# A row-mean kernel read in tiles: 126 rows a partition in place of 127, and a second block of 128 rows behind the second tile

## The chip, the cores and the metric

The kernel runs on one core of one Trainium2 chip. The metric is device time in microseconds of the whole program; a profile's span is about 1.3 us shorter (159.8 us for a run of 161.13 us in the kernel before). The engines in the profile are DVE (VectorE), ACT (ScalarE), POOL (GpSimd) and SP (SyncE, which issues the DMA transfers); TensorE does nothing here.

## The reference

```python
batch, seq, dim = 32, 512, 1024           # x: 16384 rows of 1024 float32, 64 MiB
def reference(x):
    return np.mean(np.maximum(x, 0), axis=-1).astype(np.float32)
```

Each row of 4 KB becomes one number. There is one pass over 64 MiB and next to no output (64 KB).

## The kernel before

The first 128 rows are a block by themselves, one row a partition. The other 16256 are dealt out 127 to a partition, so that a partition's rows are contiguous in HBM. They come in seven tiles of 16 rows a partition, then in ever smaller pieces (7, 4, 2, 1 rows, and the last row in three pieces of columns), so that little work is left behind the last byte. Three buffers take the tiles in turn.

```python
xfirst, xmain = xf[:P, :], xf[P:, :]
J = J - 1                                            # 127
xr = xmain.rearrange("(p j) d -> p j d", p=P, j=J)
NB, BUFS = 16, 3
row_pieces, col_pieces = [7, 4, 2, 1], [512, 256, 256]
# ... cut ...
for t in range(full):                                # full = 7, on SP
    buf_free(t)            # from t = 3 on: ACT and DVE are through with tile t - 3
    if t == 0:
        load(-1, row0[:, :], xfirst)
    load(t, bufs[t % BUFS][:, :, :], xr[:, t * NB:(t + 1) * NB, :])
    if t == BUFS:
        nc.sync.wait_ge(first, 2)
        nc.sync.dma_start(
            out=outfirst.rearrange("(q i) -> q i", i=32), in_=turned0[0:P:32, :],
        ).then_inc(stored, 16)
# ... cut: loads of the row and column pieces ...
def rows(i, xt, lo, n, j0):
    nc.scalar.wait_ge(loaded[i], 16)
    nc.vector.wait_ge(loaded[i], 16)
    for k in range(lo, lo + n):
        j = j0 + k
        done = (dve_row if j % 2 else act_row)(nc, xt[:, k, :], sums[:, j:j + 1])
        # ... cut: the last two rows of a tile count up dve and act ...
# ... cut ...
nc.scalar.wait_ge(loaded[-1], 16)
nc.scalar.activation(
    out=row0[:, :], in_=row0[:, :], func=ACT.Relu, scale=inv, accum_out=mean0[:, 0:1],
).then_inc(first, 1)
nc.vector.wait_ge(first, 1)
nc.vector.transpose(turned0[:, :], mean0[:, :]).then_inc(first, 1)
for t in range(full):
    rows(t, bufs[t % BUFS], 0, NB, t * NB)
```

Odd rows go to DVE and even rows to ACT, each with one instruction that takes the maximum with 0 and sums up (for a row, 1.22 us on DVE and 1.04 us on ACT in the profile before). The means of the block lie one in each partition; a transpose of 32 x 32 blocks (0.21 us on DVE) turns them into four rows of 32 numbers, which a small store of 4 x 128 B writes out (four packets of 128 B in the trace).

## Time and profile before

| what | before |
|---|---|
| time, median of the first 3 runs (lowest to highest) | 161.34 us (161.02 to 161.39) |
| span of the profiled run | 159.8 us |
| busy: DVE, ACT | 46%, 44% |
| HBM read | 67.11 MB, 420 GB/s over the span |
| from tile to tile (8.39 MB) | 19.34 to 19.36 us, 433 GB/s |
| last DVE operation starts | 157.84 us |

The prediction shows the lines that carry this. In the DMA row each digit is a fortieth of the span in tenths busy; in a group's line, the figures behind the second bar are the engine's idle time ahead of that group and what ended it. In a line of the timeline, square brackets hold the engine's wait just before the instruction and what ended it. One more view belongs in front: what SP issued, in order. Columns are start, length, engine and line, operation, what is written from what, and how many were merged. The first three lines show the block, then tiles 0 to 3, then the small store behind tile 3 (tiles count from 0); the last shows the final store.

```profile
0.00 0.39 SPq L109 DMA_DIRECT2D row<-in_x_dram  x1
0.45 32.18 SPq L109 DMA_DIRECT2D rows<-in_x_dram  x4
32.68 0.64 SPq L125 DMA_DIRECT2D out_dram<-turned  x1
...
158.30 0.34 SPq L208 DMA_DIRECT2D out_dram<-res  x1
```

### The profile page before, as it was taken

What the parts mean: (1) busy time and instruction counts of PE and PEld (TensorE: products, weight loads), DVE (VectorE), ACT (ScalarE), POOL (GpSimd) and SP (SyncE); (2) the same over time, 40 slices, a digit from 0 to 9 for tenths busy, and PEclk for the clock granted to TensorE, in tenths of its full rate; (3) what the DMA queues carried; (4) which work ended last, traced back from release to release, by engine and by line L of the source; (5) the groups of instructions that cost most, each with busy time, mean ns of one, the idle gap of its engine ahead of it and who ended that gap; (6) DMA issues with size and microseconds to landing.
All of it is one profiled execution on the core that took longest, in us unless ns stands there. A gap on an engine that the chain in (4) does not pass through costs nothing. (4 is left out here: it accounts for less than half of the span.)

```text
span 159.8 us, 348 instructions
## 1 busy us (share of the span) xinstructions
DVE 73.3 (46%) x131; ACT 70.4 (44%) x133; POOL 1.3 (1%) x9
## 2 busy tenths in 40 slices
DVE  0000029900399005970079500894009920199975
ACT  1400029800397005950079300892009900199974
POOL 1000000000000000000000000000000000000001
DMA  9979989999799699699699699799899997998993
GB/s 394 459 328 525 410 377 525 394 394 525 345 443 525 263 525 525 263 525 525 263 525 509 279 525 476 312 525 427 361 525 394 394 525 328 427 438 382 414 411 110
DMA packets 2456, 67.18 MB, mean 420 GB/s; under 512 B 536, under 2 KB 792, under 8 KB 1176
## 3 DMA queue, kind: packets, MB, share of 16 engines
q1 hardware_dynamic: 2456, 67.18, 97.9%
HBM read 67.11 MB, written 0.07 MB: 420 GB/s over the span
## 5 line engine op out<-in xcount | busy, mean ns | idle before, releaser
L20 DVE TENSOR_SCALAR_CACHE_REDUCE rows<-rows 128x1024 f32<-128x1024 f32 (+1 forms) x63 | 72.1, 1209 | 78.8 <-DMA rows<-in_x_dram 78.6
L15 ACT ACTIVATE rows<-rows 128x1024 f32<-128x1024 f32 x64 | 66.2, 1035 | 84.0 <-DMA rows<-in_x_dram 83.8
L15 ACT ACTIVATION_READ_ACCUMULATOR rows<-rows 128x1 f32 x64 | 11.9, 186 | 0.0
L20 DVE DVE_READ_ACCUMULATOR rows<-rows 128x1 f32 x63 | 5.2, 83 | 0.0
L168 DVE STREAM_TRANSPOSE turned<-mean 128x32 f32<-128x32 f32 x1 | 0.2, 211 | 5.9 <-ACT row L164 5.9
L164 ACT ACT_TABLE_LOAD x1 | 1.3, 1283 | 3.3 <-DMA row<-in_x_dram 3.3
L157 POOL TENSOR_SCALAR res<-sums 128x112 f32<-128x112 f32 (+1 forms) x2 | 0.5, 249 | 153.8 <-DVE rows L20 153.8
L164 ACT ACTIVATE row<-row 128x1024 f32<-128x1024 f32 x1 | 1.1, 1056 | 0.0
L15 ACT ACTIVATE last<-last 128x512 f32<-128x512 f32 x1 | 0.6, 629 | 0.0
L20 DVE TENSOR_SCALAR_CACHE_REDUCE last<-last 128x256 f32<-128x256 f32 x1 | 0.4, 420 | 0.3 <-DMA last<-in_x_dram 0.3
L197 DVE SCALAR_TENSOR_TENSOR last<-last,scale 128x258 f32<-128x258 f32 x1 | 0.4, 428 | 0.1
L142 POOL MEMSET scale<- 128x258 f32 x1 | 0.3, 313 | 0.0
L187 POOL TENSOR_SCALAR res<-part 128x1 f32<-128x1 f32 x1 | 0.3, 266 | 0.6 <-DVE rows L20 0.6
L164 ACT ACTIVATION_READ_ACCUMULATOR row<-row 128x1 f32 x1 | 0.2, 187 | 0.0
L15 ACT ACTIVATION_READ_ACCUMULATOR last<-last 128x1 f32 x1 | 0.2, 186 | 0.0
L141 POOL MEMSET mean<- 128x32 f32 x1 | 0.1, 125 | 1.5 <-POOLq L55 1.5
L235 POOL MEMSET const-bfloat16-1.0<- 128x1 bf16 x1 | 0.1, 103 | 0.0
L235 POOL MEMSET const-uint8-127<- 128x1 uint8 x1 | 0.1, 103 | 0.0
L235 POOL MEMSET const-float32-0.0<- 128x1 f32 x1 | 0.1, 99 | 0.2 <-issue 0.2
L235 POOL MEMSET const-float32-1.0<- 128x1 f32 x1 | 0.1, 99 | 0.0
L20 DVE DVE_READ_ACCUMULATOR last<-last 128x1 f32 x1 | 0.1, 83 | 0.0
L197 DVE DVE_READ_ACCUMULATOR last<-last,scale 128x1 f32 x1 | 0.1, 82 | 0.0
## 6 DMA issues: line engine op xcount, KB each, us to landing
rows<-in_x_dram SPq DMA_DIRECT2D x1, 3584.0 KB, 37.9
rows<-in_x_dram SPq DMA_DIRECT2D x1, 2048.0 KB, 42.4
rows<-in_x_dram SPq DMA_DIRECT2D x1, 1024.0 KB, 44.5
row<-in_x_dram SPq DMA_DIRECT2D x1, 512.0 KB, 3.2
rows<-in_x_dram SPq DMA_DIRECT2D x1, 512.0 KB, 45.3
last<-in_x_dram SPq DMA_DIRECT2D x1, 256.0 KB, 45.5
last<-in_x_dram SPq DMA_DIRECT2D x2, 128.0 KB, 45.2
rows<-in_x_dram SPq DMA_DIRECT2D x7, 48.7
```

The costliest lines, as they stand in the source:

```text
L15: return nc.scalar.activation(out=src, in_=src, func=ACT.Relu, accum_out=acc)
L20: return nc.vector.tensor_scalar(out=src, in0=src, scalar1=0.0, scalar2=init, op0=ALU.max, op1=ALU.add, accum_out=acc,)
L141: nc.gpsimd.memset(mean0[:, :], 0.0)
L142: nc.gpsimd.memset(scale[:, :], inv).then_inc(pool, 1)
L157: nc.gpsimd.tensor_scalar(out=res[:, lo:hi], in0=sums[:, lo:hi], scalar1=inv, scalar2=0.0, op0=ALU.mult, op1=ALU.add,).then_inc(pool, 1)
L164: nc.scalar.activation(out=row0[:, :], in_=row0[:, :], func=ACT.Relu, scale=inv, accum_out=mean0[:, 0:1],).then_inc(first, 1)
L168: nc.vector.transpose(turned0[:, :], mean0[:, :]).then_inc(first, 1)
L187: nc.gpsimd.tensor_scalar(out=res[:, J - 2:J - 1], in0=part[:, 0:1], scalar1=part[:, 1:2], scalar2=inv, op0=ALU.add, op1=ALU.mult,).then_i ...
L197: nc.vector.scalar_tensor_tensor(out=last[:, 768:], in0=last[:, 768:], scalar=0.0, in1=scale[:, :], op0=ALU.max, op1=ALU.mult, accum_out=r ...
L235: nc = _bacc.Bacc("TRN2", target_bir_lowering=False, num_devices=1)
```

## The change

A second block of 128 rows is taken out of the front, so 126 rows a partition remain (504 KiB from one partition's rows to the next in HBM, before 508 KiB). The second block is loaded behind tile 1 and worked on by ACT between tiles 1 and 2. The first tail piece has 6 rows in place of 7, the last store 14 columns in place of 15, and there are two small stores, behind tile 5.

```diff
-    xfirst, xmain = xf[:P, :], xf[P:, :]
-    J = J - 1
+    xfirst, xmain = xf[:2 * P, :].rearrange("(c p) d -> p c d", c=2), xf[2 * P:, :]
+    J = J - 2
-    row_pieces = [7, 4, 2, 1]
+    row_pieces = [6, 4, 2, 1]
     for t in range(full):
         buf_free(t)
-        if t == 0:
-            load(-1, row0[:, :], xfirst)
+        if t in (0, 2):
+            c = t // 2
+            load(c - 2, row0[:, c, :], xfirst[:, c, :])
         load(t, bufs[t % BUFS][:, :, :], xr[:, t * NB:(t + 1) * NB, :])
-        if t == BUFS:
+        if t == BUFS + 2:
             nc.sync.wait_ge(first, 2)
-            nc.sync.dma_start(... one store of 4 x 32 ...).then_inc(stored, 16)
+            for c in range(2):
+                nc.sync.dma_start(... one store of 4 x 32 ...).then_inc(stored, 16)
     for t in range(full):
+        if t in (0, 2):
+            c = t // 2
+            nc.scalar.wait_ge(loaded[c - 2], 16)
+            done = nc.scalar.activation(
+                out=row0[:, c, :], in_=row0[:, c, :], func=ACT.Relu, scale=inv, accum_out=mean0[:, c:c + 1],
+            )
+            if c == 1:
+                done.then_inc(first, 1)
+                nc.vector.wait_ge(first, 1)
+                nc.vector.transpose(turned0[:, :], mean0[:, :]).then_inc(first, 1)
         rows(t, bufs[t % BUFS], 0, NB, t * NB)
# ... cut: the same activation and transpose removed from ahead of the loop;
#     one semaphore more; the wait for all stores is 64 in place of 48 ...
```

More of the change, by code (lines that the diff above doesn't have):

```diff
@@ L63 @@
     inv = 1.0 / D
-    xfirst, xmain = xf[:P, :], xf[P:, :]
-    outfirst, outmain = out.flatten()[:P], out.flatten()[P:]
-    J = J - 1
+    xfirst, xmain = xf[:2 * P, :].rearrange("(c p) d -> p c d", c=2), xf[2 * P:, :]
+    outfirst, outmain = out.flatten()[:2 * P], out.flatten()[2 * P:]
+    J = J - 2
     xr = xmain.rearrange("(p j) d -> p j d", p=P, j=J)
@@ L88 @@
     scale = sbuf("scale", P, D // 4 + 2)
-    row0, mean0, turned0 = sbuf("row0", P, D), sbuf("mean0", P, 32), sbuf("turned0", P, 32)
-    loaded = [nc.alloc_semaphore(f"loaded{i}") for i in range(full + len(row_pieces) + len(col_pieces) + 1)]
+    row0, mean0, turned0 = sbuf("row0", P, 2, D), sbuf("mean0", P, 32), sbuf("turned0", P, 32)
+    loaded = [nc.alloc_semaphore(f"loaded{i}") for i in range(full + len(row_pieces) + len(col_pieces) + 2)]
     act, dve, pool = (nc.alloc_semaphore(n) for n in ("act", "dve", "pool"))
@@ L118 @@
         buf_free(t)
-        if t == 0:
-            load(-1, row0[:, :], xfirst)
+        if t in (0, 2):
+            c = t // 2
+            load(c - 2, row0[:, c, :], xfirst[:, c, :])
         load(t, bufs[t % BUFS][:, :, :], xr[:, t * NB:(t + 1) * NB, :])
-        if t == BUFS:
+        if t == BUFS + 2:
             nc.sync.wait_ge(first, 2)
-            nc.sync.dma_start(
-                out=outfirst.rearrange("(q i) -> q i", i=32), in_=turned0[0:P:32, :],
-            ).then_inc(stored, 16)
+            for c in range(2):
+                nc.sync.dma_start(
+                    out=outfirst[c * P:(c + 1) * P].rearrange("(q i) -> q i", i=32), in_=turned0[c:P:32, :],
+                ).then_inc(stored, 16)
     j0 = full * NB
@@ L162 @@
     nc.vector.wait_ge(pool, 1)
-    nc.scalar.wait_ge(loaded[-1], 16)
-    nc.scalar.activation(
-        out=row0[:, :], in_=row0[:, :], func=ACT.Relu, scale=inv, accum_out=mean0[:, 0:1],
-    ).then_inc(first, 1)
-    nc.vector.wait_ge(first, 1)
-    nc.vector.transpose(turned0[:, :], mean0[:, :]).then_inc(first, 1)
-    for t in range(full):
+    for t in range(full):
+        if t in (0, 2):
[8 more added lines that the diff above has]
+                nc.vector.transpose(turned0[:, :], mean0[:, :]).then_inc(first, 1)
         rows(t, bufs[t % BUFS], 0, NB, t * NB)
@@ L212 @@
     nc.sync.sem_clear(range(used[0], used[-1] + 1))
-    nc.sync.wait_ge(stored, 48).then_inc(stored, -48)
+    nc.sync.wait_ge(stored, 64).then_inc(stored, -64)
     for e, hint in zip(hinted, hints):
```

## The prediction

The sum came to +0.10 us (161.34 + 0.10, stated as 161.45). One of the two grounds for its 0.08 us is the one-row piece of the tail, 1.28 us behind the piece before it where its bytes take 1.21, so read the 0.08 as the author's estimate from this 0.07. The "6.5 us around it" are 161.34 less the 154.8 us of the input. The 16 and the 8 in the packet count are worked out from the trace before: it has 276 packets of 4 B, which comes to 16 for each of the 15 loads and the two stores of 128 packets, and 4 for the small store, beside that store's 4 of 128 B.

> **What bounds the kernel now.** I read the page from the top, then the waits, then the busy time between tile arrivals, then the last four microseconds of the timeline. The page first: neither compute engine is half used, the DMA row is full from the first slice to the last but one, and both compute groups spend more time waiting for rows than working on them.
>
> ```profile
> span 159.8 us, 348 instructions
> DVE 73.3 (46%) x131; ACT 70.4 (44%) x133; POOL 1.3 (1%) x9
> DMA  9979989999799699699699699799899997998993
> ...
> DMA packets 2456, 67.18 MB, mean 420 GB/s; under 512 B 536, under 2 KB 792, under 8 KB 1176
> ...
> L20 DVE TENSOR_SCALAR_CACHE_REDUCE rows<-rows 128x1024 f32<-128x1024 f32 (+1 forms) x63 | 72.1, 1209 | 78.8 <-DMA rows<-in_x_dram 78.6
> L15 ACT ACTIVATE rows<-rows 128x1024 f32<-128x1024 f32 x64 | 66.2, 1035 | 84.0 <-DMA rows<-in_x_dram 83.8
> ```
>
> The reader is to see 78.6 us of idle DVE and 83.8 us of idle ACT, all ended by the arrival of x. The kernel is a stream of 64 MiB, and the engines keep up. The chain of waits (the page's part 4) names only the last DVE instruction, because a landing is not an instruction, so it doesn't help here.
>
> Next, busy time by stage, with the cuts put where each tile of 16 rows a partition is first touched, that is, where it landed:
>
> ```profile
> 22.99:42.35 19.36, 9.21 (x16) 8.42 (x16) 0.00 (x0) 1.00 1.00 433
> 42.35:61.71 19.36, 9.21 (x17) 8.43 (x17) 0.00 (x0) 1.00 1.00 433
> 61.71:81.05 19.34, 9.21 (x16) 8.42 (x16) 0.00 (x0) 1.00 1.00 434
> 81.05:100.40 19.35, 9.21 (x16) 8.42 (x16) 0.00 (x0) 1.00 1.00 434
> ```
>
> The columns are the stretch, its length, busy time of DVE, ACT and POOL with counts, the granted clock, the DMA share and GB/s. Each tile is 128 x 16 x 4096 B = 8.39 MB, and 8.39 MB / 19.355 us = 433.4 GB/s with a DMA share of 1.00: not one gap between tiles. One row a partition (512 KiB) therefore costs 19.355 / 16 = 1.210 us of stream, and the whole input 128 x 1.210 = 154.8 us out of a time of 161.34. What is left is the start (first bytes), the work behind the last bytes, the last store, and some 1.3 us outside the span (the profiled run had a span of 159.8 and a time of 161.13).
>
> Last, the end of the timeline (start, length, engine, operation):
>
> ```profile
> 152.51 1.22 DVE L20 TENSOR_SCALAR_CACHE_REDUCE rows<-rows 128x1024 f32<-128x1024 f32 x1 [0.77 <-DMA rows<-in_x_dram]
> ...
> 156.29 0.75 DVE L20 TENSOR_SCALAR_CACHE_REDUCE rows<-rows 128x576 f32<-128x576 f32 x1
> ...
> 157.32 0.42 DVE L20 TENSOR_SCALAR_CACHE_REDUCE last<-last 128x256 f32<-128x256 f32 x1 [0.27 <-DMA last<-in_x_dram]
> ...
> 157.84 0.43 DVE L197 SCALAR_TENSOR_TENSOR last<-last,scale 128x258 f32<-128x258 f32 x1
> 158.19 0.08 DVE L197 DVE_READ_ACCUMULATOR last<-last,scale 128x1 f32 x1
> 158.30 0.34 SPq L208 DMA_DIRECT2D out_dram<-res  x1
> ```
>
> Right up to the last column pieces DVE waits for data (0.77 us before the piece of four rows, 0.27 us before the columns 512 to 767). Behind the last bytes come one short DVE operation, the issue of the store (0.34 us) and 1.0 us until it has landed.
>
> [...] tiles become usable in the order of issue, 19.34 to 19.36 us apart.
>
> **The change part by part.** (1) Bytes of x: unchanged. Before: 1 block row + 7 x 16 + 7 + 4 + 2 + 1 + 1 = 128 rows a partition. After: 1 + 32, 1, 5 x 16, then 6 + 4 + 2 + 1 + 1 = 128. So 0 us of stream added or removed.
>
> (2) Order: block two sits in the queue behind tile 1 and ahead of tile 2. Tiles 2 to 6 land 1.21 us later each (61.71 becomes about 62.9, 139.12 about 140.3), and the shortened piece (6 rows in place of 7) gives it all back: its last byte is number 120 of 128 in both kernels, so everything from 147.6 us on lands when it did. 0 us.
>
> (3) One more load in the stream, 128 packets of 4 KB[...]. What a separate DMA costs beyond its bytes I take from two places: [...] the one-row piece of the tail, which starts 156.29 - 155.01 = 1.28 us behind the piece before it in place of 1.21, 0.07 more. I add 0.08 us on the path.
>
> (4) Compute: ACT still does 64 block or whole rows (62 even rows and 2 blocks, before 63 and 1), DVE still 62, and one transpose of 0.21 us each. Block two costs ACT 1.06 us, between tile 1 and tile 2, where it idles 10.93 us. DVE waits for it and for the transpose there, and idles 10.15 us. Nothing on the path. Releases of buffers do not move, as tile 1's rows come first.
>
> (5) The tail on DVE. Tile 6 now lands at about 140.4. Eight rows at 1.14 us start to start (139.12, 140.26, ...) end at 149.5; three rows of the piece of six end at 152.9, against a landing of the next piece at 152.5 to 152.6, so the wait of 0.77 us vanishes. Two rows end at 155.2 (landed at 155.1), one at 156.4 (the one-row piece lands at 156.3 to 156.4), its 576 columns at about 157.15, and the columns 512 to 767 land at about 157.4. DVE is in step again with 0.2 us to spare, before the last operation. 0 us. ACT at 1.04 us a row ends earlier still and has one row less in that piece.
>
> (6) Stores: two of 4 x 128 B in place of one, on the fifth tile in place of the third. The old one, issued at 32.68, left no mark on any tile interval (19.34 to 19.36). I put 0.02 us on the second. The issue of about 0.64 us lies in a stretch where the SP queue has more than a tile queued. The last store has still 128 packets, of 56 B in place of 60: 0 us. One semaphore more and a wait for 64 in place of 48: 0 us.
>
> Sum: 0 + 0 + 0.08 + 0 + 0 + 0.02 + 0 = +0.10 us, so 161.34 + 0.10 = 161.44, stated as 161.45.
>
> **The rivals.** First rival: the address pattern matters. 504 KiB is 8 x 63 KiB where 508 KiB is 4 x 127 KiB, so the starts of the partitions fall on half as many residues of a power of two.[...] I give 5% to a loss that counts.
>
> Second rival: the tail becomes bound by DVE, as part (5) leaves it 0.2 us. If rows took 1.16 in place of 1.14 us, the 14 rows from tile 6 on would end 0.3 us later and the end would slip by about 0.1. In the other direction nothing is won, as the last bytes set the end. The time would be 161.6.
>
> Third rival: the first store is queued behind loads[...]; the second store doubles that. If each were worth a whole extra load, 0.08 us, it is 161.5.
>
> Fourth rival, a win: a pitch of 56 B rows on 504 B boundaries makes the last store land faster. Its whole landing takes 1.0 us now; a tenth off is 0.1, so 161.35.
>
> **Range and chances.** The three runs of before span 161.02 to 161.39, so a median can be off by 0.2 alone. The small rivals move the time between 161.2 and 161.7. The range that should hold it 8 times in 10 is 160.9 to 162.1, widened upward for a mild loss of stream rate (0.3% is 0.5 us). Faster by over 2% means under 158.1:[...] the 6.5 us around it would have to halve, which nothing in the diff does: chance 0.01. Slower by over 2% means over 164.6, which takes the first rival: 0.05. Within 2%: 0.94.
>
> **What would show it.** The DMA row should stay at 9 and the busy stretches between tile landings at 433 GB/s, with landings at about 22.99, 42.35, 62.9, 82.3, 101.6, 121.0 and 140.4; the one gap that is longer, by 1.2 to 1.3 us, is from tile 1 to tile 2. Packets should rise to 2456 + 128 + 16 + 8 = 2608, those under 512 B to 560. ACT should show one more block activation soon after 51.5, and DVE's wait before the piece of four rows should be gone while that before the columns 512 to 767 stays at about 0.2 us. The last DVE operation should start at 157.9. I am wrong if the intervals of 16 rows leave 19.35 by more than 0.1 us (then it is the pitch), if DVE has no wait left before the last columns (then the tail binds), or if the time behind the last DVE operation (1.5 us) changes by over 0.2 us (then it is the stores).

## The result, and the profile after

| | before | after |
|---|---|---|
| median of 6 runs of the same rounds | 161.23 us (161.02 to 161.53) | 161.11 us (161.05 to 161.69) |
| ratio, with 95% interval | | 0.9996 (0.9979 to 1.0014): same |

A ratio here and below is the mean time of one kernel's fast runs over that of the kernel before in the same rounds, so it is not quite the quotient of the medians beside it.

The page of the changed kernel, same parts as in the prediction:

```profile
span 159.8 us, 350 instructions
DVE 73.1 (46%) x131; ACT 70.3 (44%) x133; POOL 1.3 (1%) x9
DMA  9969979899996997998979979969969969899993
...
DMA packets 2608, 67.18 MB, mean 420 GB/s; under 512 B 560, under 2 KB 816, under 8 KB 1328
```

Nothing of weight moved. The packet counts are the 2608 and 560 that were predicted, so the change does to the stream what the reading of the diff said.

Busy time between first uses of the tiles (stretch, its length, busy DVE, ACT, POOL, clock, DMA share, GB/s):

```profile
42.23:62.88 20.65, 9.42 (x18) 9.47 (x19) 0.00 (x0) 1.00 1.08 469
62.88:82.22 19.34, 9.20 (x16) 8.42 (x16) 0.00 (x0) 1.00 1.00 434
82.22:101.58 19.36, 9.21 (x16) 8.42 (x16) 0.00 (x0) 1.00 1.00 433
```

The stretch with the second block is 1.3 us longer, and the tiles read at the new pitch come as they did: 19.34 to 19.36 us.

The issues of SP, and below them the tail, which answers to the last fence of the prediction:

```profile
0.44 1.81 SPq L109 DMA_DIRECT2D rows<-in_x_dram  x2
2.29 0.43 SPq L109 DMA_DIRECT2D row<-in_x_dram  x1
2.77 69.71 SPq L109 DMA_DIRECT2D rows<-in_x_dram  x4
72.54 1.20 SPq L127 DMA_DIRECT2D out_dram<-turned  x2
```

```profile
151.69 1.22 DVE L20 TENSOR_SCALAR_CACHE_REDUCE rows<-rows 128x1024 f32<-128x1024 f32 x1
152.49 1.06 ACT L15 ACTIVATE rows<-rows 128x1024 f32<-128x1024 f32 x1 [0.67 <-DMA rows<-in_x_dram]
152.83 1.21 DVE L20 TENSOR_SCALAR_CACHE_REDUCE rows<-rows 128x1024 f32<-128x1024 f32 x1
...
157.32 0.42 DVE L20 TENSOR_SCALAR_CACHE_REDUCE last<-last 128x256 f32<-128x256 f32 x1 [0.29 <-DMA last<-in_x_dram]
...
157.84 0.43 DVE L203 SCALAR_TENSOR_TENSOR last<-last,scale 128x258 f32<-128x258 f32 x1
```

ACT shows that the piece of four rows landed at 152.49, as before. DVE no longer waits for it (the bracket with 0.77 us is gone): it is still busy with the piece of six. It is in step again at the last columns, with 0.29 us to spare, and the last operation starts at 157.84 in both kernels.

One finer reading is needed for the experiments. Each load counts up its semaphore by 16, and the trace records the counts with their times: every load has 16 separate landings. Each of the two small stores, of four packets, has one entry at its issue (73.55 and 74.16) and four landings (120.64 to 120.75 and 120.82 to 120.93). The page counts 16 DMA engines, so I read a load's 16 landings as one from each; this is my reading, as the records don't name the engine and no run tests it. What is said below is said of the landings. Sorted out of the trace's records (us, first and last of the 16):

```
                 before             after
block 0       2.86    3.23       3.01    3.39
tile 0       22.42   22.97      22.41   22.87
tile 1       41.77   42.33      41.77   42.23
block 1                         43.05   43.52
tile 2       61.12   61.69      62.39   62.85
tile 6      138.56  139.10     139.81  140.26
last columns 157.16 157.60     157.19  157.60
```

In these two profiles the sorted landings keep their distances: first and last are 0.55 us (before) and 0.46 us (after) apart at tile 0, and 0.54 and 0.45 us at tile 6. The kernel goes on only when the last of them has landed: in the kernel before, that is at 22.97 for tile 0, and ACT and DVE start on it at 22.99.

### The profile page after: what moved, and what is told of

Read it like the earlier page. It is cut to its first block, busy times and chain, and to the rows that moved or that the text cites. A ratio compares the mean times of both kernels' runs of the same rounds, so it can differ in the third digit from the quotient of the medians.

```text
span 159.8 us, 350 instructions
## 1 busy us (share of the span) xinstructions
DVE 73.1 (46%) x131; ACT 70.3 (44%) x133; POOL 1.3 (1%) x9
## 2 busy tenths in 40 slices
DMA packets 2608, 67.18 MB, mean 420 GB/s; under 512 B 560, under 2 KB 816, under 8 KB 1328
## 3 DMA queue, kind: packets, MB, share of 16 engines
q1 hardware_dynamic: 2608, 67.18, 97.8%
## 5 line engine op out<-in xcount | busy, mean ns | idle before, releaser
L15 ACT ACTIVATE rows<-rows 128x1024 f32<-128x1024 f32 (+1 forms) x63 | 65.2, 1035 | 83.9 <-DMA rows<-in_x_dram 83.8
L169 ACT ACTIVATE row<-row 128x1024 f32<-128x1024 f32 x2 | 2.1, 1047 | 0.0
```

The source lines that it names most:

```text
L15: return nc.scalar.activation(out=src, in_=src, func=ACT.Relu, accum_out=acc)
L169: done = nc.scalar.activation(out=row0[:, c, :], in_=row0[:, c, :], func=ACT.Relu, scale=inv, accum_out=mean0[:, c:c + 1],)
```

## The experiments

Every kernel is the changed kernel with the edit shown, timed in five rounds against the kernel before; each has one profile, of one execution. "Spread" below is the last of the 16 landings of a load minus the first.

### e1_both_first: undo the place of the second block

```diff
-        if t in (0, 2):
-            c = t // 2
+        for c in (0, 1) if t == 0 else ():
             load(c - 2, row0[:, c, :], xfirst[:, c, :])
 # the same for the activation; three loads in place of two ahead of the first barrier
```

> The changed kernel with one part undone: both blocks of 128 rows come first, and ScalarE and VectorE deal with both at the start. Theory (the end is set by the last byte of 64 MiB, and the order of the loads in front of the tail is free): the first tile lands 1.21 us later (about 24.1 in place of 22.9 to 23.0), tile 2 where it was (about 62.9), and the end does not move: ratio to the kernel before 0.998 to 1.002. Rival (placing the second block late hides something at the start, such as its activation or its transpose): 0.5 us or more slower, ratio 1.003 or above.

Measured: 162.27 us (161.91 to 162.74) against 161.37, ratio 1.0055 (1.0038 to 1.0073). Neither the theory nor the rival as it was put holds. The time is lost, but not through the activation or the transpose (ACT is through with both blocks at 6.9 us and then waits 18.6 us for tile 0):

```profile
25.46 1.06 ACT L15 ACTIVATE rows<-rows 128x1024 f32<-128x1024 f32 x1 [18.60 <-DMA rows<-in_x_dram]
```

Tile 0 comes at 25.46 in place of 24.1. Fourteen of its 16 landings lie within 0.46 us, one is 0.85 and one 1.67 us behind the first (23.78 to 25.44); tile 6 still has a spread of 1.55 us. So one or two of the sixteen parts of the load came about a microsecond late at tile 0, and nothing gave it back. All sixteen landings lost a further 0.25 us between tiles 1 and 2 (the sorted landings of the two are 19.54 to 19.71 us apart in place of 19.36). The profiled run was the slowest of the six.

### e9_both_first_n2: the same, with two early loads

The edit is that of e1 without its last part: the two blocks go ahead of the program's first barrier (the point at its start where the engines wait for each other), and tile 0 behind it, issued at 1.92 us where e1 issued it at 0.91.

> e1_both_first lost 0.9 us (ratio 1.0055), which my theory had not expected; its trace has one of 16 landings of the first tile 0.8 us behind the next, and it stays so to the end. e1 also issued three loads ahead of the program's first barrier in place of two. This is e1 with two. If the third early issue was the cause, ratio 0.998 to 1.002; if it is the order of the loads (4 KB packets of two blocks at the start), 1.004 to 1.008 again.

Measured: 161.76 us (161.41 to 162.05) against 161.25, ratio 1.0029 (1.0012 to 1.0047). That is between the two expectations. The order of the loads costs some 0.5 us by itself. The third early issue may have cost the rest in e1, but the intervals of the two ratios overlap, so that is not shown. Tile 0 has fifteen landings within 0.41 us and one at 0.78 us, again kept to the end.

### e10_behind_tile0: the second block one tile earlier

```diff
-        if t in (0, 2):
-            c = t // 2
+        if t in (0, 1):
+            c = t
```

> The changed kernel with the second block behind tile 0 in place of tile 1. If only the very start is touchy (two blocks of 4 KB packets ahead of the first big packets), this is like the changed kernel, ratio 0.998 to 1.002, and all 16 landings of tile 0 lie within 0.6 us. If a block of 4 KB packets between large ones sets engines apart wherever it comes early, the landings of tile 1 spread to over 0.8 us and the ratio is 1.002 or more.

Measured: 161.33 us (161.06 to 161.73) against 161.25, ratio 1.0002 (0.9984 to 1.0021); the spread of tile 0 is 0.45, of tile 1 0.46 us. Behind one tile of large packets the block does no harm that the times show; of the three places tried, only the very start cost time. The landings can also draw apart later: in this profile the spread grows from 0.45 us at tile 3 to 0.66 us at tile 6, well behind the block, and the mean of the 16 landings takes 77.63 us from tile 2 to tile 6, where the changed kernel took 77.41. The profiled executions of e1 (above) and e2 (below, 77.70 us) also lost 0.2 us or more in mid-stream; the cause is open. Why a landing or two of tile 0 fall behind when the first 1 MiB is two blocks (by 0.78 us in e9, 0.85 and 1.67 us in e1) stays open: it was seen in both profiles, and its cause wasn't separated further.

### e2_pitch512: the partitions 512 KiB apart

```diff
-    xr = xmain.rearrange("(p j) d -> p j d", p=P, j=J)
+    xr = xf.rearrange("(p j) d -> p j d", p=P, j=J + 2)[:, 2:, :]   # wrong result on purpose
```

The size that the rival had here came from figures which no run of this case shows, and is cut; so is what the theory gave as its cause.

> The changed kernel with one size changed: each partition's 126 rows are taken from rows p*128+2 on, so that partitions lie 512 KiB apart in HBM in place of 504 KiB. Same bytes, same packets; the result is wrong on purpose. Theory[...]: intervals between tiles stay at 19.35 us, ratio 0.998 to 1.002. Rival (the pitch matters, and 508 and 504 were both merely good choices):[...]

Measured: 161.45 us (161.33 to 161.98) against 161.37, ratio 1.0008 (0.9992 to 1.0023).

```profile
42.83:63.45 20.62, 9.42 (x17) 9.47 (x18) 0.00 (x0) 1.00 1.05 455
63.45:83.09 19.64, 9.20 (x16) 8.43 (x16) 0.00 (x0) 1.00 1.00 427
83.09:102.45 19.36, 9.21 (x16) 8.42 (x16) 0.00 (x0) 1.00 1.00 433
```

The rate is that of the other pitches but for one interval, and the ratio leaves room for a loss of 0.23% at most, so the rival falls: among 504, 508 and 512 KiB the pitch doesn't set the rate of these loads. One interval of 19.64 and a spread of 0.97 us at tile 0 (1.12 us at tile 6) may hint that the landings draw apart more easily here, but this profile was the slowest of the six runs, and the times don't tell the pitches apart.

### e4_no_block2: 512 KiB less

```diff
-        if t in (0, 2):
-            c = t // 2
+        if t == 0:
+            c = 0
             load(c - 2, row0[:, c, :], xfirst[:, c, :])
 # and no activation for c == 1; 128 results wrong on purpose
```

> The changed kernel without the second block: neither loaded nor worked on (128 results wrong on purpose). It takes 512 KiB of 64 MiB out of the stream, ahead of the tail. Theory (bytes set the end): 1.21 us faster plus at most 0.08 for the load as such, 159.9, ratio 0.992. Rival (the tail on VectorE or the stores set the end): VectorE is nearly back to back through the tail in the changed kernel and would be still, so the end would move by the same only if VectorE waits for bytes; if it did not, less than 0.6 us is won, ratio 0.996 or above.

Measured: 159.94 us (159.85 to 160.54) against 161.37, ratio 0.9922 (0.9903 to 0.9941), as the theory has it. The last DVE operation starts at 156.60, 1.24 us earlier than in the changed kernel:

```profile
156.09 0.42 DVE L20 TENSOR_SCALAR_CACHE_REDUCE last<-last 128x256 f32<-128x256 f32 x1 [0.28 <-DMA last<-in_x_dram]
```

DVE's wait of 0.28 us ahead of the last columns is still there. Bytes taken out of the stream come out of the time in full.

### e3_split16: tiles 1 to 6 in sixteen loads each

```diff
-        load(t, bufs[t % BUFS][:, :, :], xr[:, t * NB:(t + 1) * NB, :])
+        step = 1 if 1 <= t <= 6 else NB
+        for k in range(0, NB, step):
+            load(t, bufs[t % BUFS][:, k:k + step, :], xr[:, t * NB + k:t * NB + k + step, :])
 # rows() waits for 256 in place of 16 there
```

> The changed kernel with tiles 1 to 6 each loaded as sixteen loads of one row a partition: 90 loads more, same bytes, packets of 4 KB in place of larger ones. It measures the 0.08 us that the prediction charged for a separate load. If a load costs 0.08 us of stream: 90 x 0.08 = 7.2 us, tiles 20.6 us apart, time about 168.3, ratio 1.044. If separate loads behind each other in the queue are free: tiles 19.35 us apart, ratio 1.00. A value between gives the true cost of a load: (time - 161.2) / 90.

Measured: 168.32 us (168.29 to 168.34) against 161.37, ratio 1.0433 (1.0416 to 1.0451). That is 7.0 us for 90 loads, 0.08 us each, the size the prediction had charged. But each load also came with 128 packets of 4 KB, and the next run parts the two.

### e7_packets4k: one load a tile, in packets of 4 KB

```diff
+        src = xr[:, t * NB:(t + 1) * NB, :]
+        if 1 <= t <= 6:
+            a = NB * (t - (t - 1) % 2)
+            src = xr[:, a:a + 2 * NB, :].rearrange("p (k two) d -> p k two d", two=2)[:, :, (t - 1) % 2, :]
+        load(t, bufs[t % BUFS][:, :, :], src)     # wrong result on purpose
```

> e3_split16 took 7.1 us more for 90 more loads, but its data also went in packets of 4 KB in place of 64 KB. This kernel parts the two: tiles 1 to 6 are one load each as in the changed kernel, but a tile takes every second row of 32 (the next tile takes the others), so each row of 4 KB is a run, and a packet, of its own; rows land in other places, so the result is wrong on purpose. If the number of packets costs, 11520 of e3's 12960 more packets are here, and the time is about 167.5, ratio 1.039. If the load as such costs[...], ratio 1.000 to 1.003.

Measured: 167.96 us (167.89 to 167.98) against 161.25, ratio 1.0412 (1.0396 to 1.0428).

```profile
DMA packets 14128, 67.18 MB, mean 403 GB/s; under 512 B 560, under 2 KB 816, under 8 KB 13616
```

```profile
65.12:85.60 20.48, 9.21 (x16) 8.43 (x16) 0.00 (x0) 1.00 1.03 410
85.60:106.08 20.48, 9.21 (x16) 8.42 (x16) 0.00 (x0) 1.00 1.03 410
```

The packets cost, and the load as such costs next to nothing: e3's tiles were 20.48 to 20.57 us apart with sixteen loads each, these are 20.48 with one. A tile has 2048 packets of 4 KB in place of 128 of 64 KB. Dealt out evenly to the 16 engines, which the records don't show, that is 120 more on each, so a packet costs by estimate (20.48 - 19.355) / 120 = 9.4 ns beyond its bytes. A packet of 4 KB is here also a separate run of 4 KB in HBM, so these runs don't part the packet from the shorter run. The intervals of e3's and e7's ratios overlap, but the traces show what the loads cost on top: from tile 1 to tile 6 the mean of the 16 landings (in e3 of a tile's last load) moves by 103.71 us in e3 and by 103.68 in e7. So 75 further loads, each with 16 landings of its own, took 0.03 us. The medians are 0.36 us apart, and so are the last landings of tile 0, ahead of any split tile (23.22 and 22.86): e3 seems to lose its time at the start.

### e5_stores16: the small stores in sixteen parts

Two stores of 4 x 128 B become sixteen of 4 x 16 B (repeating the whole stores would have been a race between writes of the same bytes).

```diff
-            for c in range(2):
+            for c, h in [(c, h) for c in range(2) for h in range(0, 32, 4)]:
                 nc.sync.dma_start(... [:, h:h + 4] of both sides ...).then_inc(stored, 16)
```

> The changed kernel with each of the two small stores cut into eight of 4 x 16 B: sixteen small stores in place of two, in the middle of the stream; the result is right. If a small store in the stream costs what the prediction charged (0.02 us), 14 more cost 0.28 us, ratio 1.002; if each costs as much as a load was charged (0.08 us), 1.1 us, ratio 1.007; if they are lost among the loads, nothing, and no interval between tiles differs from 19.35 by over 0.05.

Measured: 162.95 us (162.75 to 163.10) against 161.22, ratio 1.0104 (1.0087 to 1.0120): more than any of the three expectations. The interval from tile 5 to tile 6, between whose loads the stores are issued, is 21.16 us in place of 19.35. The landings tell how: the spread is 0.30 us at tile 5 and 1.75 us at tile 6, with twelve landings within 0.41 us and exactly four at 1.65 to 1.75. The twelve are late too: the first landing of tile 6 is 19.73 us behind the first of tile 5, and the mean of all 16 landings is 0.83 us late, where four landings, each at most 2.1 us late, would make 0.53.

### e8_stores16_far: sixteen stores of the real size

```diff
+            for c in range(2, 16):
+                nc.sync.dma_start(
+                    out=outmain[c * P:(c + 1) * P].rearrange("(q i) -> q i", i=32), in_=turned0[c:P:32, :],
+                ).then_inc(stored, 16)
 # the main store, which overwrites these, waits for them
```

> Sixteen small stores again, but each is 4 x 128 B as in the changed kernel, to its own 512 B of the output (fourteen of them are overwritten by the main store, which waits for them; the result is right). In e5_stores16 four of the 16 landings of tile 6 came 1.3 us or more behind the other twelve. Theory: a small store holds up the four DMA engines it runs on by 0.10 us each, and shows in the time only beyond what these are ahead of the slowest one, so the time is again 162.7 to 163.0, ratio 1.010. Rival: in e5 it was stores of 16 B into the same 128 B that held each other up; then far less is lost here, ratio below 1.004, and two stores cost nothing at all.

Measured: 162.85 us (162.73 to 163.10) against 161.25, ratio 1.0098 (1.0083 to 1.0113), so the rival (that stores into the same 128 B are the cause) falls as an account of the lost time.

```profile
101.59:120.97 19.38, 9.20 (x16) 8.43 (x16) 0.00 (x0) 1.00 1.03 433
120.97:142.07 21.10, 9.21 (x17) 8.43 (x17) 0.00 (x0) 1.00 0.91 394
```

Again twelve landings of tile 6 lie within 0.39 us and four at 2.04 to 2.17. As many landings as a small store has come some 1.6 to 2.1 us late, and the whole tile with them; the landings of the stores themselves follow each other at 0.17 us from store to store. (The range is open because the sorted landings don't tell where these four stood among the 0.43 us at tile 5.) The mean of all 16 landings is 0.49 us late; if the other twelve lost nothing, the four lost 2.0 us each. That these four belong to the engines that carry the stores is my reading; no record names them. The first landing is on time here (19.35 us). Why the twelve were late in e5, with as many stores, wasn't tested. Yet the two stores of the changed kernel had left the sorted landings of tiles 5 and 6 alike to 0.02 us.

### e11_stores6_far: six of them

The edit is that of e8 with `range(2, 6)`.

> As e8_stores16_far, with six small stores in place of sixteen. In e8 the stores of one engine land 0.17 us apart, 16 x 0.17 = 2.75 us, but the four engines came out of it only about 1.8 us late, and in the changed kernel two stores left no trace at all. Theory A (an engine makes up for about 0.95 us, some five or six stores, before any shows): the landings of tile 6 keep their spread (under 0.6 us), ratio 0.998 to 1.002. Theory B (every store holds its engines up by 0.11 us from the first on, and two were merely hidden in these engines' lead): four engines 0.66 us later at tile 6 than at tile 5, of which at most 0.45 can lie in their lead; ratio 1.001 to 1.004, spread of the landings over 0.6 us.

Measured: 161.11 us (161.03 to 161.13) against 161.17, ratio 0.9994 (0.9981 to 1.0008). The spread was 0.36 us at tile 5 and 0.24 us at tile 6, so theory B falls: 0.66 us on four of the landings couldn't have stayed within it. A, that nothing shows at all, is nearly right: the last landing came 19.38 us after that of tile 5 in place of 19.35, and the two earliest landings of tile 5 have no counterpart at tile 6, so at least two of the sixteen lost 0.1 us or more, none more than 0.39 us. By the mean of the landings (0.07 us late), the four lost 0.28 us each for six stores, again if the others lost nothing. From six to sixteen that is (2.0 - 0.28) / 10 = 0.17 us for each further store, the distance at which they land, and below 0.05 us for each of the first six. These are estimates from one profile each. That the cost doesn't grow in proportion to the number is shown; what makes the first ones cheap is not.

### e6_dve_plus_row: one row more for DVE in tile 6

```diff
-            done = (dve_row if j % 2 else act_row)
+            done = (dve_row if j % 2 or j == 100 else act_row)
```

> The changed kernel with one of the 62 rows of ScalarE (row 100, in tile 6) given to VectorE, 1.14 us of work. VectorE is busy 46% of the span, so by the average this is free (ratio 1.000). My theory says otherwise: from tile 6 on VectorE waits for bytes only 0.29 us, before the last columns. So its last columns start about 1.14 - 0.29 = 0.85 us later and the end moves by as much: ratio 1.005, the last VectorE operation at about 158.7 in place of 157.84. Undone the other way, in the kernel before VectorE had more to spare there (0.77 + 0.27 us).

Measured: 161.96 us (161.86 to 162.72) against 161.22, ratio 1.0050 (1.0031 to 1.0068).

```profile
158.15 0.42 DVE L20 TENSOR_SCALAR_CACHE_REDUCE last<-last 128x256 f32<-128x256 f32 x1
158.41 0.27 POOL L193 TENSOR_SCALAR res<-part 128x1 f32<-128x1 f32 x1 [0.49 <-DVE rows L20]
158.67 0.43 DVE L203 SCALAR_TENSOR_TENSOR last<-last,scale 128x258 f32<-128x258 f32 x1
```

The bracket at the last columns is gone: DVE is late for them, and the last operation starts 0.83 us later. An engine busy for 46% of the span had 0.29 us to spare where it mattered.

### e12_dve_minus_row: one row less

```diff
+            done = (dve_row if j % 2 and j != 101 else act_row)
```

> The counterpart of e6_dve_plus_row: row 101 of tile 6 goes from VectorE to ScalarE in the changed kernel. VectorE then has 1.14 us more room in the tail, ScalarE 1.04 us less, of the 0.67 + 0.31 us that it waits there. Theory (the last bytes set the end, the room that the change took from VectorE cost nothing): last VectorE operation at 157.8 to 157.95, ratio 0.999 to 1.002. Rival (in the changed kernel VectorE sets the end of the tail in part): the last operation starts 0.1 us or more earlier relative to the last landing.

Measured: 161.05 us (160.96 to 161.22) against 161.17, ratio 0.9990 (0.9976 to 1.0003).

```profile
152.55 1.22 DVE L20 TENSOR_SCALAR_CACHE_REDUCE rows<-rows 128x1024 f32<-128x1024 f32 x1 [0.71 <-DMA rows<-in_x_dram]
...
157.91 0.43 DVE L203 SCALAR_TENSOR_TENSOR last<-last,scale 128x258 f32<-128x258 f32 x1
```

DVE has its wait ahead of the piece of four rows back, and the end doesn't come earlier: the last landing was at 157.71, so the last operation starts 0.20 us behind it, in the changed kernel 0.24 (157.84 against 157.60). So the room that the change took from DVE had cost nothing that the times show. No kernel that does the whole work beats the two beyond the noise.

## Why the prediction was right

The predicted 161.45 us and "within 2%" hold; the measured median is 161.11. Step by step:

1. **Bytes set the end: right, and tested both ways.** Taking 512 KiB out moved the time by 0.8% (e4), and giving DVE more room moved nothing (e12). The pitch did nothing to the rate at 504 KiB (19.34 to 19.36 us a tile, as at 508), nor, but for one interval of 19.64 us, at 512 (e2, ratio 1.0008), so the first rival falls. What sets these 433 GB/s is not shown.
2. **Order: right for the change, wrong as a general statement.** Tile 2 landed at 62.85 (predicted about 62.9), tile 6 at 140.26 (about 140.4), the tail where it was. But e1 and e9 show that order is not free at the very start, where 0.5 to 0.9 us were lost.
3. **0.08 us for a further load: right in size, and it is the packets.** Block 1 landed 1.29 us behind tile 1 (43.52 - 42.23), where its bytes take 1.21; by the mean of the 16 landings it is 1.27 to 1.29 us in all nine profiles in which the block lies there (the changed kernel, e2, e3, e5 to e8, e11, e12). Its 128 packets of 4 KB, eight on each engine if dealt out evenly, make 0.075 us at e7's 9.4 ns (an estimate from e7). What was wrong is the name: a separate load as such costs nothing that these runs resolve (75 of them 0.03 us, e3 against e7).
4. **Compute: right**, but for one time. ACT took the second block at 50.6 us, not soon after 51.5: it had ended tile 1 earlier than DVE, whose end I had used. DVE waited 0.29 us for the transpose, at a place where it waits for tile 2 anyway.
5. **The tail on DVE: right.** The wait of 0.77 us vanished, 0.29 us were left where 0.2 had been worked out, the last operation started at 157.84 (157.9). e6 moved it by 0.83 us for 0.85 expected.
6. **Stores: right by luck.** The 0.02 us stood for a small effect of every store. There is a large effect on four landings of the next tile for sixteen stores (1.6 to 2.1 us, e8), but none for two (within 0.02 us) and little for six (0.07 us in the mean, e11). The third rival's 0.08 us a store would have been wrong for two and too little for sixteen. The fourth rival, a faster last store, shows nothing: issued at 158.30 in both kernels, its last part landed at 159.75 before and 159.76 after.

The sum of +0.10 us is not to be seen in the times, and should not be expected to be: the last landing of tile 0 came 0.10 us earlier in the profile of the changed kernel than in that of the kernel before (22.87 and 22.97), and over the profiles of kernels that start alike (e4 to e8, e10 to e12) it lies between 22.74 and 22.97. What the start happens to give is as large as the whole sum, and the interval of the ratio is 0.0035 wide, 0.56 us. The landings do show it, once the start is taken off: from tile 0 to the last columns the mean of the 16 landings takes 134.69 us in the kernel before, 134.79 in the changed kernel and 134.78 in e6, whose loads are the same. That is 0.09 us for the 0.10 predicted. (In e12, also with the same loads, it takes 134.86, but 0.08 of this was lost between tiles 0 and 1, ahead of the block; so a single execution can stray by nearly the whole sum.)

## What to carry to other kernels

When a stream of loads runs without gaps, as here, ask four things of a change: does it alter the bytes, the number of packets, the work behind the last byte, or the pace of any of the 16 parts that a load lands in? Moving the block to behind tile 0 or tile 1 cost nothing that the times show. Read the slack of an engine at the place where the end is set, not from its busy share. And look at all the landings of a load, not only at the last of them: what one or two of them lost at the start stayed to the end (e1, a spread of 1.55 us at tile 6; e9), while a delay of at most 0.39 us of landings that came early did not show in the time (e11, ratio 0.9994). The mean of the landings shows effects of 0.1 us that the times don't.
